# Dilated scores by two query tiles, split lows on Pool, the last head pair's weights spread by TensorE, and an earlier first load of branch weights, in a three-branch encoder block

## The chip, the cores and the metric

The kernel runs on one core of a Trainium2 chip. The profile names its engines: TensorE (PE, with its weight loads as PEld), VectorE (DVE), ScalarE (ACT), GpSimd (POOL, here "Pool") and SyncE (SP), which here only issues DMA. Each takes its own instructions in order; they wait for each other through semaphores. The metric is device microseconds of one execution, as the median of several runs. All data are float32. Matrix products that have to be exact are made as three products of a value's high and low part (h*h, h*l, l*h): a "split" is one ScalarE copy that rounds to the high part, and one subtraction that leaves the low part.

## The reference, cut to what matters

One block over 1024 tokens of width 1024. `h = rms_norm(x)`, one wide projection, three mixers, each gated by a SiLU and projected back, merged by sigmoid gates, projected by `w_out`, normalised and added to `x`. The change lies in the first mixer and in the products that run beside it:

```python
for gi, (window, dil) in enumerate(((128, 1), (512, 4), (2048, 16))):
    o_g, lse_g = dilated_window_attention(aq[gi], ak[gi], av[gi], window, dil)   # 8 heads of 64
wts = softmax(stack(lses), axis=0)                # over the three groups, per token and head
oa  = einsum('gbsh,gbshd->bshd', wts, stack(outs))
ya = (oa * silu(ga)) @ w_br_a
yb = (ob * silu(gb)) @ w_br_b
ym = (om * silu(gm)) @ w_br_m
merged = gates[0] * ya + gates[1] * yb + gates[2] * ym
x = x + rms_norm(merged @ w_out)
```

In each group a query sees the keys at `t + j*dil` with `|j| <= window/(2*dil)`: after sorting tokens by class modulo `dil`, a band of 64 to each side, or, in the third group, all 64 tokens of its class.

## The kernel before, in words

The program runs in stages: projections and cross-attention, grouped-query attention, the values, then the rotated queries and keys together with the merge gates (25 "pairs" of column blocks), then the dilated stage, the first branch's products, and the output projection. The change touches the end of the fourth stage, all of the dilated stage, and the way into the products after it.

**Order.** Every engine's order in these stages is written out by hand: it is the order in which the Python code emits instructions. `weave` (around line 180) mixes two generators: the dense work of `run_items` and an attention generator. Each yields a cost. After each yield it goes on with the dense side if the attention's share `a / att_cost` has reached the dense share `d / dc`, else with the attention. In the dilated stage the dense work is 16 units of 24 matmuls (`add_y`, units 0 to 7 the cross-attention branch, 8 to 15 the grouped-query branch), `dc` = 384 x 216. `att_cost` is the last line of the stage's pacing (`weave(16, every(), ...)`): 7000 + 12 x 9500 + 5000 + 33000 = 159000. The constants stand at the bottom: SOFT 1000, JOINED 300, LAG 3, FIRST_PAD 7000, LAST_PAD 1000. Small pieces of a unit wait in the list `pend`, one popped every third matmul: at a unit's start the load of the next unit's gate (`th_load`), the load of the weights of the unit after it (`y_load`), and the next unit's weight split (`y_split`, high part on ScalarE L1335, low part on Pool L1336); at the end of each half the evacuation (`y_evac`: VectorE L1351 or L1353 out of the PSUM bank `d`, of which there are two, and for units from 8 on an addition on Pool, L1354).

**A cycle.** There are four head pairs and three groups, so twelve items, in the order pair 0 group 0, 1, 2, pair 1 group 0, and so on; an item's cycle has eight steps T, one for each tile of 128 queries. `plan` writes a cycle as a list of pieces. At each step: `soft(T)` (VectorE L1564 adds the mask to the scores in PSUM and takes the minimum of the negated scores, ScalarE L1565 makes the exponential and its sum), `trans(T - 3)` (TensorE transposes the probabilities, VectorE copies them to `app`, L1603 or L1578), a piece of the combination of an earlier pair (`combining`), and loads or splits (`tokens`). `scores(0)` makes the scores of tiles 0 to 3 in the four `s1` banks (two heads, two tiles in a bank), `scores(1)` those of tiles 4 to 7. `joined` puts `scores(1)` behind the previous item's second `pv` at step 3, and the next item's `scores(0)` behind the own first `pv` at step 7. `pv` multiplies with the values into a PSUM bank, and ScalarE copies to `og` (L1632; four buffers). At step 2 `stats` transposes the previous item's minima and sums, and eight or four DMAs (L1647 to L1658) store them to `std` in DRAM, sorted by class.

**Combining a pair.** When a pair's third item is finished, `ready` (step 3 of the next cycle) starts `combine`: `fetch` reads the pair's statistics from `std`, `shares` and `weights` make the softmax over the groups on small tiles, `put` stores it to `wgd`, `get` reads it back spread over 64 rows for each head (`wgt`), `weigh` multiplies each group's `og` and adds them up (Pool, L1796 and L1798), `gate` multiplies with 0.5 and the SiLU gate (VectorE, L1801), `store` keeps or stores the result. `STEP_T` gives the step of each piece, shares first, counted on through the following cycles. For the last pair there is no following cycle: `ending` makes the same pieces one after the other on VectorE, with the DMAs on ScalarE's queue, and then splits the result into `hh[3]` and `hl[3]`.

**The low parts.** The grouped-query branch's operands are loaded and split during the second to sixth cycle (`b_load`, `b_high` L1832, `b_low` L1836 on VectorE); those of the dilated branch that are ready (pairs 0, 1, 2) in the last cycle (`dl_high` L1843, `dl_low` L1846 on VectorE).

**Into and out of the stage.** In the last pass of the loop over the 25 pairs (`n == last`), SP issues `op_load(hi)` (eight loads of the cross-attention operands; four of them take buffers from `kr`, a rotation of ten), `qk_first`, then `y_load(0)`. `c_add` and `c_fin` take more `kr` buffers for the merge gates that end there. After `weave`, units 16 to 18 run with the first three operand tiles (`y_part(m, range(3))`, L1944), then with the fourth.

## Time and profile before

| | |
|---|---|
| median of 3 runs | 1467.03 us (1465.35 to 1470.9) |
| the profiled execution | 1466.1 us, its span 1464.3 us |
| busy share of the span | PE 95%, PEld 76%, DVE 71%, ACT 45%, POOL 41% |
| chain of waits, by engine | PE 75%, DVE 6%, DMA 6%, POOL 5%, issue 3%, ACT 2%, SP's queue 2% |
| `soft` on VectorE, L1564 | 192 instructions, mean 323 ns |
| `soft` on ScalarE, L1565 | 192 activations, mean 422 ns, each with an accumulator read of 187 ns |
| first `soft` starts, last `soft` starts | 1079.3 us, 1275.9 us |
| last unit of `add_y`, first `y_part` matmul | 1319.1 us, 1326.3 us |

The page cuts the span into 40 slices of 36.6 us; a digit is the busy share of a slice in tenths. In a list of groups the columns are: line, engine, operation, tiles written and read, shapes, count; busy us and mean ns of one; idle time just before them and what ended it. In an order of time a line starts with start and duration in us; what stands in brackets is how long the engine was idle before, and what released it. In a list of waits: who waited, for whom, us in all, times, the longest.

### The profile page before, as it was taken

The page shows a single profiled execution, that of the slowest core. Times are in us where ns is not written, and L with a number is a line of the kernel's source. Part 1 is how long each engine was busy: PE and PEld are TensorE (multiplying, and loading weights), DVE is VectorE, ACT ScalarE, POOL GpSimd, SP SyncE. Part 2 cuts the span into 40 slices and gives each one's busy share as a digit, 9 for nine tenths or more (in the row PEclk, how much of TensorE's full clock was granted, in tenths as well). Part 3 has the DMA queues.
Part 4 walks back from the last instruction along what each step waited for, and adds up shares of the span by engine and source line. Part 5 has one row for each costly group of instructions (what it writes and reads, how often), then busy time and mean ns, then how long its engine had stood idle before and what let it go on. Part 6 is the DMA issues. An engine that isn't in the chain of part 4 may idle for free.

```text
span 1464.3 us, 21835 instructions
## 1 busy us (share of the span) xinstructions
PE 1386.2 (95%) x7768; PEld 1113.6 (76%) x7768; DVE 1034.6 (71%) x1805; ACT 659.7 (45%) x1377; POOL 601.3 (41%) x457
## 2 busy tenths in 40 slices
PE   7999999999999999999999999999979898939897
PEld 7799986666666889888888888888857676727786
DVE  7768678677762887677787766777856665644977
ACT  6544366666554453333333333333346555502332
POOL 1416604676654003445555544555400424625303
PEclk9999999999999999999999999999989999979999
DMA  6347432232203795142333333333555676653355
GB/s 237 100 159 260 142 115 94 79 98 89 74 25 123 236 285 175 69 145 82 113 108 115 115 107 109 115 101 119 176 213 184 198 203 213 168 145 120 135 213 173
DMA packets 121341, 209.74 MB, mean 143 GB/s; under 512 B 33616, under 2 KB 62096, under 8 KB 121232
## 3 DMA queue, kind: packets, MB, share of 16 engines
q1 hardware_dynamic: 110160, 192.75, 41.3%
q10 hardware_dynamic: 11072, 15.59, 3.1%
q8 instruction: 61, 1.00, 0.3%
q14 instruction: 48, 0.39, 0.1%
HBM read 143.97 MB, written 64.32 MB: 142 GB/s over the span
## 4 chain that ended last, share of the span: by engine, by line
PE 75%; DVE 6%; DMA 6%; POOL 5%; issue 3%; ACT 2%; SPq 2%; DVEq 0%; ACTq 0%; POOLq 0%
PE s L1298 32%; PE s L1210 4%; PE s L2030 4%; PE ov L797 3%; PE s L1259 3%; PE d L145 3%; PE d L143 3%; PE d L147 3%; PE d L1859 2%; PE s L782 2%; PE s L781 2%; PE tr L763 2%; PE d L2030 1%; DMA wgt<-wgd 1%; PE d L538 1%
## 5 line engine op out<-in xcount | busy, mean ns | idle before, releaser
L788 POOL TENSOR_TENSOR bl<-bl,bp 128x512 f32<-128x512 f32 x96 | 130.8, 1362 | 54.3 <-ACT bp L784 48.9
L1298 PE MATMUL s<-hh,vS 128*128 128x512 f32 x400 | 133.6, 395 | 0.0
L1298 PE MATMUL s<-vA,vS 128*128 128x512 f32 x450 | 106.6, 390 | 0.0
L1565 ACT ACTIVATE pra<-pra,sts 128x192 f32<-128x192 f32 (+2 forms) x192 | 80.8, 422 | 54.4 <-DVE sts L1564 47.0
L106 DVE TENSOR_TENSOR vS<-vot,vS 128x512 fp32r<-128x512 f32 x75 | 85.6, 1143 | 19.9 <-ACT vS L105 19.9
L1298 PEld LDWEIGHTS s<-vA,vS 128*128 128x128 f32 x450 | 84.5, 188 | 18.3
L784 ACT ACTIVATE bp<-s 128x512 f32<-128x512 f32 x128 | 75.8, 596 | 43.2 <-PE s L782 42.2
L764 DVE TENSOR_REDUCE bn<-tr 128x1 f32<-128x512 f32 x128 | 84.8, 683 | 12.0 <-PE tr L763 10.8
L143 PE MATMUL d<-hh,wh 128*128 128x512 f32 x224 | 89.3, 399 | 2.4 <-DVE fth L216 2.4
L147 PE MATMUL d<-hh,wl 128*128 128x512 f32 x224 | 89.4, 399 | 0.0
L1298 PEld LDWEIGHTS s<-hh,vS 128*128 128x128 f32 x400 | 75.3, 188 | 18.3 <-DVE vS L106 0.4
L145 PE MATMUL d<-hl,wh 128*128 128x512 f32 x224 | 88.9, 397 | 0.0
L1336 POOL TENSOR_TENSOR wh<-wr,wh 128x512 fp32r<-128x512 f32 x19 | 26.6, 1401 | 132.6 <-ACT wh L1335 132.6
L1564 DVE CUSTOM_DVE_ANT_0 pra<-s,mask 128x192 f32<-128x192 f32 (+2 forms) x192 | 54.6, 323 | 37.1 <-PE s L1552 17.7
L1298 PE MATMUL s<-hl,vS 128*128 128x512 f32 x200 | 79.1, 395 | 0.0
L1298 PE MATMUL s<-hh,wh 128*128 128x512 f32 x200 | 78.4, 392 | 0.0
L1298 PE MATMUL s<-hh,wl 128*128 128x512 f32 x200 | 78.4, 392 | 0.0
L1298 PE MATMUL s<-hl,wh 128*128 128x512 f32 x200 | 77.8, 389 | 0.0
L1859 PE MATMUL d<-bh,wh 128*128 128x512 f32 x128 | 47.5, 435 | 25.1 <-DVE wl L1353 25.1
L1302 ACT ACTIVATE vv<-s 128x512 f32<-128x512 f32 x50 | 30.0, 599 | 86.0 <-PE s L1298 58.1
L1354 POOL TENSOR_TENSOR acc<-acc,wl 128x512 f32<-128x512 f32 (+1 forms) x23 | 41.2, 1794 | 48.7 <-DVE wl L1353 48.5
L797 PE MATMUL ov<-bp,VS 128*64 128x512 f32 x256 | 58.5, 598 | 0.0
(591 smaller groups left out, 4082.7 us busy)
## 6 DMA issues: line engine op xcount, KB each, us to landing
wr<-in_wu SPq DMA_DIRECT2D x40, 512.0 KB
vA<-in_wu SPq DMA_DIRECT2D x24, 512.0 KB
qkd<-ko SPq DMA_DIRECT2D x96, 128.0 KB
wl<-thd SPq DMA_DIRECT2D x24, 512.0 KB
wos<-os SPq DMA_DIRECT2D x12, 512.0 KB
aq<-qkd SPq DMA_DIRECT2D x12, 512.0 KB
ak<-qkd SPq DMA_DIRECT2D x12, 512.0 KB
wr<-in_wbr SPq DMA_DIRECT2D x24, 256.0 KB
```

The source lines that it names most:

```text
L106: V.tensor_tensor(dst_l, src, dst_h.bitcast(F32), op=OP.subtract)
L143: PE.matmul(dst, wh[:, k, :], hh[k][:, t], start=k == 0, stop=False)
L145: PE.matmul(dst, wh[:, k, :], hl[k][:, t], start=False, stop=False)
L147: PE.matmul(dst, wl[:, k, :], hh[k][:, t], start=False, stop=k == 7)
L764: fp["last"] = V.tensor_reduce(st[i]["n"][:, j, c:c + 1], s, axis=AX.X, op=OP.min)
L784: A.activation(pp, s, AF.Exp, scale=-1.0)
L788: G.tensor_tensor(lsum[i % 2], lsum[i % 2], pp, op=OP.add)
L797: PE.matmul(o[e * 64:e * 64 + 64], VS[:, kt, kv], d.pop(kt), start=kt < 2, stop=kt >= NT - 2)
L1298: PE.matmul(BANK[n, c], a, b, start=k == 0 and q == 0 and not more, stop=k == 3 and q == 2, skip_group_check=c in "XW")
L1565: A.activation(src, src, AF.Exp, scale=-1.0, bias=bias, accum_out=sts[:, h, 1, T:T + 1])
L1859: PE.matmul(ps_, a, b, start=k == 0 and q == 0, stop=k == 3 and q == 2)
L2030: PE.matmul(dst[:, e[0]:e[1]], a, b, start=k == 0 and q == 0, stop=k == 3 and q == 2)
```

## The change

- **Scores.** `scores` makes two tiles a call. The four calls stand at step 5 and 7 of the cycle before (tiles 0 to 3) and at steps 1 and 3 of the own cycle; `joined` is gone, and the costs are divided.
- **Lows and gates.** `b_low` and `dl_low` (but for the last operand) move from VectorE to Pool, `b_high` and `dl_high` go by halves, spread over the steps of a cycle. `gate` of pairs 0 to 2 moves to Pool; its factor 0.5 goes into `weights`. In `STEP_T`, `get` goes from step 0 of the next cycle to step 7, the gate from step 4 to step 1.
- **The last pair.** Its third item writes its statistics straight into `c3`. Those of the first two are read back from DRAM by four loads into `rows` at step 6 of the last cycle, transposed by TensorE into `c3`. `shares_3` makes the softmax over groups, transposes it to 48 rows (group, head, tile), and multiplies it with a 0/1 pattern into a 48 x 1024 tile. `wide` spreads it to 128 rows by a matmul with a second 0/1 pattern; `first_two` and `third` multiply the `og` tiles with it out of PSUM by halves of 512, add them and apply the gate, on VectorE. The last `stats`, `fetch`, `put` and `get` are gone.
- **Pacing.** `att_cost` becomes 136000 (33000 -> 10000), and the padding of the last steps is halved.
- **The first load.** `y_load(0)` stands ahead of `op_load(hi)`. In the last pair of column blocks, `c_add` and `c_fin` take other buffers than those of `kr`.

```diff
@@ c_add, c_fin
-        r = RV[n, u, t] = kr()
+        r = RV[n, u, t] = kr() if n < last or n == last and (u, t) == (0, 0) else SF[(1 - u) * 2]
...
-        r = kr() if ps_ is not None else RV.pop((n, u, t))
+        r = RV.pop((n, u, t)) if ps_ is None else kr() if n < last else p1
@@ the loop over pairs, n == last
+            y_load(0)
             op_load(hi)
             op_split(lo, 0)
             op_split(lo, 1)
...
             qk_first(0)
-            y_load(0)
             th_load(0)
@@ new constants
+        def pickers():
+            i48 = ident[0:48, 0:48]
+            V.tensor_reduce(pick, i48.rearrange("p (x t) -> p t x", t=NT), axis=AX.X, op=OP.add)
+            V.tensor_reduce(each, i48.rearrange("p (x t) -> p x t", t=NT), axis=AX.X, op=OP.add)
+            V.tensor_copy(spread.rearrange("p g h q -> p (g h) q"), each[:, :, None].to_broadcast([48, 6, 64]))
@@ scores
-                    d["sts"] = cb.tile([P, 2, 2, NT], F32, name="sts", bufs=2)
+                    d["sts"] = c3[:, 2] if (p_, g) == (3, 2) else cb.tile([P, 2, 2, NT], F32, name="sts", bufs=2)
-                for j in range(4):
-                    T = 4 * b + j
+                banks = [pss1(), pss1()]
+                for j in range(2):
+                    T = 2 * b + j
@@ tokens
+                if (n, T) == (1, 7):
+                    pickers()
+                if 2 <= n <= 5 and 4 <= T <= 6:
+                    (lambda: b_high(n - 2, lo), lambda: b_high(n - 2, hi), lambda: b_low(n - 2))[T - 4]()
...
+                if n == 11:
+                    if T < 6:
+                        k, z = divmod(T, 3)
+                        dl_high(k, half[z]) if z < 2 else dl_low(k)
+                    else:
+                        dl_high(2, half[T - 6])
                     if T == 4:
-                        DL["g"] = qk.tile([P, S], F32, name="aq", bufs=2)
+                        DL["g"] = cb.tile([P, S], F32, name="wgt", bufs=3)
...
+                        for j in range(4):
+                            nc.sync.dma_start(rows[16 * j:16 * j + 16],
+                                              std[3, j % 2, j // 2].rearrange("s (t a) -> (s t) a", t=NT))
@@ plan
+                if T == 1 and it:
+                    out.append(it["scores"][2])
+                if T == 5 and nxt:
+                    out.append(nxt["scores"][0])
                 if T == 3:
-                    out.append(joined(pre and pre["pv"][1], it and it["scores"][1]))
+                    if pre:
+                        out.append(pre["pv"][1])
                     if it:
+                        out.append(it["scores"][3])
...
                 if T == 7:
-                    out.append(joined(it["pv"][0], nxt and nxt["scores"][0]))
+                    out.append(it["pv"][0])
                     if nxt:
+                        out.append(nxt["scores"][1])
@@ combine
-            def gate(g, gt):
-                V.scalar_tensor_tensor(ogs[g], ogs[g], 0.5, gt, op0=OP.mult, op1=OP.mult)
+            def gate():
+                G.tensor_tensor(ogs[0], ogs[0], c["g"], op=OP.mult)
...
-        STEP_T = (6, 7, 7, 0, 3, 3, 7, 4, 5)
+        STEP_T = (6, 7, 7, 7, 3, 3, 7, 1, 5)
@@ b_low, dl_low
-            V.tensor_tensor(l, l.bitcast(F32), h.bitcast(F32), op=OP.subtract)
+            G.tensor_tensor(l, l.bitcast(F32), h.bitcast(F32), op=OP.subtract)
...
-            V.tensor_tensor(hl[k][:, t], DL[k][:, t], hh[k][:, t].bitcast(F32), op=OP.subtract)
+            (V if k == 3 else G).tensor_tensor(hl[k][:, t], DL[k][:, t], hh[k][:, t].bitcast(F32), op=OP.subtract)
@@ the last pair (shares_3's softmax over groups cut: the same small operations as shares and weights)
+                PE.transpose(tp[:, 0, 0:64], rows, ident[0:64, 0:64])
+                V.tensor_copy(c3[:, 0:2].rearrange("p g h s t -> p (g h s t)"), tp[:, 0, 0:64])
...
+                PE.transpose(tp[0:48, 0, :], C["e"].rearrange("p g h t -> p (g h t)"), ident)
+                C["w"] = wv = cb.tile([P, S], F32, name="wgt", bufs=3)
+                for x in range(2):
+                    t = slice(32 * x, 32 * x + 32)
+                    V.tensor_tensor(wv[0:48, half[x]].rearrange("p (u t z) -> p u t z", t=NT, z=2),
+                                    tp[0:48, 0, :].rearrange("p (z u) -> p u z", z=2)[:, t, None, :].to_broadcast([48, 32, NT, 2]),
+                                    pick[:, None, :, None].to_broadcast([48, 32, NT, 2]), op=OP.mult)
+        def wide(g, x):
+            W3B[g, x] = pst().rearrange("p a b -> p (a b)") if g == 2 else pss1()
+            PE.matmul(W3B[g, x], spread[:, g].rearrange("p h q -> p (h q)"), C["w"][0:48, half[x]], start=True, stop=True)
+        def first_two(x):
+            t = half[x]
+            a, b = C["ogs"]
+            for g, z in enumerate((a, b)):
+                V.tensor_tensor(z[:, t], W3B[g, x], z[:, t], op=OP.mult)
+            V.tensor_tensor(a[:, t], a[:, t], b[:, t], op=OP.add)
+        def third(x):
+            t = half[x]
+            a, b = C["ogs"][0], OG[3, 2]
+            V.tensor_tensor(b[:, t], W3B[2, x], b[:, t], op=OP.mult)
+            V.tensor_tensor(a[:, t], a[:, t], b[:, t], op=OP.add)
+            V.tensor_tensor(a[:, t], a[:, t], DL["g"][:, t], op=OP.mult)
@@ ending, every
+            return [(lambda: [wide(g, 0) for g in range(2)], 300.0), (lambda: [wide(g, 1) for g in range(2)], 300.0),
+                    (lambda: [first_two(0), wide(2, 0)], 1000.0), (lambda: [first_two(1), wide(2, 1)], 1000.0),
+                    (lambda: third(0), 1000.0), (lambda: dl_high(3, lo), 100.0), (lambda: third(1), 1000.0),
+                    (lambda: dl_low(3, lo), 100.0), (lambda: dl_high(3, hi), 100.0), (lambda: dl_low(3, hi), 1000.0),
+                    (out_pool, 100.0), (lambda: [wo_load(nm, k) for nm in ("B11", "B21") for k in range(4)], 500.0)]
...
-                yield cost + LAST_PAD
+                yield cost + LAST_PAD / 2
...
-        weave(16, every(), FIRST_PAD + 12 * (NT * (SOFT + 100.0) + 2 * JOINED + 100.0) + 5 * LAST_PAD + 33000.0)
+        weave(16, every(), FIRST_PAD + 12 * (NT * (SOFT + 100.0) + 2 * JOINED + 100.0) + 5 * LAST_PAD + 10000.0)
```

More of the change, by code (lines that the diff above doesn't have):

```diff
@@ L1468, in block @@
         G.memset(vpart, 0.0)
+        rows = aa.tile([64, P], F32, name="rows")
+        c3 = aa.tile([P, 3, 2, 2, NT], F32, name="c3")
+        pick = aa.tile([48, NT], F32, name="pick")
+        each = aa.tile([48, 6], F32, name="each")
+        spread = aa.tile([48, 3, 2, 64], F32, name="spread")
+        def pickers():
[3 more added lines that the diff above has]
+            V.tensor_copy(spread.rearrange("p g h q -> p (g h) q"), each[:, :, None].to_broadcast([48, 6, 64]))
         def qk_fetch(p_, g):
@@ L1887, in wo_split @@
             split(h, l, l.bitcast(F32))
[L1889 to L1903 removed]
+        C, W3B = {}, {}
```

98 lines of the change are left out of this document (45 added, 53 removed).

## The prediction

> **What bounds the kernel now.** I read the page's slices first, for where TensorE is not full; then windows around the dilated stage, for how much of it is missing there; then each engine's order of time at the two places where it stands, and the waits in between.
>
> ```profile
> span 1464.3 us, 21835 instructions
> ...
> PE   7999999999999999999999999999979898939897
> ```
>
> Slices are 36.6 us. TensorE is full until slice 28 and has one deep hole, the 3 in slice 35 (1281 to 1318). The changed code runs from about 1047 to 1345. Its windows (us; then busy time and count of TensorE, weight loads, VectorE, ScalarE, GpSimd; clock, DMA share, GB/s), and below them the branch matmuls of L1859 alone:
>
> ```profile
> 1079.30:1277.00 197.70, 177.98 (x1835) 143.76 (x1836) 124.24 (x519) 118.69 (x435) 67.07 (x34) 0.96 0.62 186
> 1277.00:1294.70 17.70, 17.07 (x101) 12.99 (x99) 11.03 (x18) 4.20 (x10) 9.52 (x7) 1.00 0.36 101
> 1294.70:1319.10 24.40, 0.00 (x0) 0.00 (x0) 10.01 (x13) 2.41 (x4) 1.29 (x2) 0.58 0.66 177
> 1319.10:1326.30 7.20, 7.16 (x25) 5.74 (x26) 1.78 (x3) 0.00 (x0) 5.41 (x4) 0.77 0.45 147
> 1326.30:1464.30 138.00, 123.91 (x541) 100.91 (x539) 105.38 (x138) 41.64 (x89) 39.41 (x34) 0.96 0.47 162
> ```
>
> ```profile
> 1079.30:1277.00 197.70, 89.52 (x268) 44.99 (x269) 0.96 0.62 186
> 1277.00:1294.70 17.70, 16.06 (x65) 11.64 (x64) 1.00 0.36 101
> 1319.10:1326.30 7.20, 7.16 (x24) 5.54 (x24) 0.77 0.45 147
> ```
>
> The twelve cycles take 197.7 us with TensorE at 90%: there it is nearly the bound. After the last softmax (1277) come 17.7 us of branch matmuls, 24.4 us of nothing, then unit 15. What ends the nothing, in VectorE's and TensorE's order of time:
>
> ```profile
> 1288.39 0.63 DVE L1769 TENSOR_TENSOR cmn<-cpt 128x16 f32<-128x16 f32 x1 [1.21 <-DMA cpt<-std]
> ...
> 1290.74 0.21 DVE L1783 TENSOR_TENSOR ceg<-ceg,cds 128x48 f32<-128x48 f32 x1
> ...
> 1301.04 1.03 DVE L1796 TENSOR_TENSOR og<-og,wgt 128x512 f32<-128x512 f32 x1 [9.50 <-DMA wgt<-wgd]
> 1306.98 1.03 DVE L1796 TENSOR_TENSOR og<-og,wgt 128x512 f32<-128x512 f32 x1 [4.90 <-DMA wgt<-wgd]
> ...
> 1318.32 0.68 DVE L1353 SCALAR_TENSOR_TENSOR wl<-wl,d 128x512 f32<-128x512 f32 x1
> ```
>
> ```profile
> 1319.14 0.76 PE L1859 MATMUL d<-bh,wh 128*128 128x512 f32 x1 [24.50 <-DVE wl L1353]
> 1319.71 0.63 PE L1859 MATMUL d<-bl,wh 128*128 128x512 f32 x1
> ```
>
> VectorE stands three times for the weights that went to DRAM and back (`put`, `get`); the evacuation L1353 of unit 14 is queued behind those multiplies, so both `d` banks stay full and TensorE stops. When it starts again its clock is low: 0.58 and 0.77 in the windows.
>
> **The change, part by part.**
>
> *Start.* `y_load(0)` goes ahead of the eight loads of `op_load(hi)` and two of `qk_first`. SP's, ScalarE's and TensorE's order of time:
>
> ```profile
> 1047.37 0.37 SPq L1318 DMA_DIRECT2D tab<-g2d  x1
> ...
> 1049.83 0.38 SPq L1318 DMA_DIRECT2D vy<-od  x1
> 1056.75 0.32 SPq L1318 DMA_DIRECT2D tab<-g2d  x1
> ...
> 1058.59 0.38 SPq L1330 DMA_DIRECT2D wr<-in_wbr  x1
> ```
>
> ```profile
> 1066.10 0.63 ACT L1335 ACTIVATE wh<-wr 128x512 fp32r<-128x512 f32 x1 [8.20 <-DMA wr<-in_wbr]
> ```
>
> ```profile
> 1066.79 0.80 PE L1859 MATMUL d<-hh,wh 128*128 128x512 f32 x1 [4.81 <-ACT wh L1335]
> ```
>
> The load would be issued at about 1047.4 and, even at the 7.5 us that this one took, be there by 1055; ScalarE is free at 1058. What is late next is the products' own end: TensorE's last one ends at 1066.79 - 4.81 = 1061.98. So unit 0 can gain at most 4.8 us; the low half on VectorE comes after a load that SP issues one slot (0.4 us) later, and I take 3.7. All that follows on VectorE and ScalarE up to the first softmax moves with it. The other buffers of `c_add` and `c_fin` cost nothing: the four that `op_load(hi)` takes are drawn earlier in the rotation, so SP's gap from 1049.83 to 1056.75 stays.
>
> *Pacing.* The constants of the interleaving give the share of branch matmuls issued by the last cycle's end: before (7000+114000)/159000 = 76%, 292 of 384 (the trace: 384-65-24 = 295). After, 121000/136000 = 89%, 342. So 47 more stand inside the cycles; at 16.06/65 = 0.247 us that is +11.6 us of TensorE. It leaves 42 for the tail.
>
> *Score blocks of two tiles.* The waits of VectorE and of TensorE's weight loads inside the cycles (total, times, longest):
>
> ```profile
> DVE pra L1564 <- PE s L1552: 17.7, 11, 2.4
> ...
> DVE pra L1564 <- PE s L1545: 12.5, 8, 2.3
> ```
>
> ```profile
> PEld tr L1624 <- DVE app L1603: 9.4, 8, 2.8
> PEld tr L1591 <- ACT og L1632: 6.1, 3, 3.0
> ...
> PEld s L1552 <- DVE sts L1564: 3.0, 2, 2.3
> ```
>
> The same matmuls run, now issued two tiles ahead of the softmax that reads them, so VectorE's 30.2 us of waits should mostly go. That is no gain by itself, since TensorE is the fuller engine; it counts where it shortens TensorE's 18.5 us above. The extra matmuls also give the others time. Bounds: nothing recovered, or all of TensorE's idle time there, 197.7 - 178.0 = 19.7 us. I take 12, most of what the rows for VectorE's lateness (9.4, 3.0) come to; the `og` wait is Pool's. Net of the cycles: about 0. VectorE's wait for the fetched statistics of pairs 0 to 2 stays as it is.
>
> *Split lows and gates on Pool.* From the groups by form between 1066 and 1320:
>
> ```profile
> L1796 POOL TENSOR_TENSOR og<-og,wgt 128x1024 f32<-128x1024 f32 x9 | 27.2, 3027 | 23.0 <-DMA wgt<-wgd 23.0
> ...
> L1336 POOL TENSOR_TENSOR wh<-wr,wh 128x512 fp32r<-128x512 f32 x15 | 21.0, 1400 | 122.7 <-ACT wh L1335 122.7
> ...
> L1798 POOL TENSOR_TENSOR og<-og 128x1024 f32<-128x1024 f32 x6 | 15.1, 2517 | 0.5
> L1351 DVE SCALAR_TENSOR_TENSOR acc<-wl,d 128x512 f32<-128x512 f32 x16 | 10.9, 679 | 0.0
> L1836 DVE TENSOR_TENSOR bl<-bl,bh 128x1024 fp32r<-128x1024 f32 x4 | 6.4, 1611 | 0.4 <-ACT bh L1832 0.4
> L1846 DVE TENSOR_TENSOR hl<-hl,hh 128x1024 fp32r<-128x1024 f32 x2 | 5.2, 2592 | 0.3 <-ACT hh L1843 0.3
> L1801 DVE SCALAR_TENSOR_TENSOR og<-og,wgt 128x1024 f32<-128x1024 f32 x3 | 3.7, 1227 | 0.0
> L1846 DVE TENSOR_TENSOR hl<-og,hh 128x1024 fp32r<-128x1024 f32 x1 | 1.3, 1299 | 0.9 <-ACT hh L1843 0.9
> ```
>
> VectorE loses 6.4 + 5.2 + 1.3 + 3.7 = 16.6 us; Pool gains four lows, three gates, three lows of the last operand, 10 x 2.5 = 25 us, on 67 in 197.7. On average there is room. Queued behind them on Pool are the weight lows L1336. One is issued at the ninth matmul of a unit and needed 15 matmuls later, some 9 us (314 matmuls in 197.7 us are 24 in 15). Where a pair's weighing (3 x 3.0 + 2 x 2.5 us) meets a low, a gate and a weight low, 20 us fall into the 12 between step 3 of one cycle and step 1 of the next, so Pool is late by up to 8: covered, with one to spare. Each us beyond that is paid at three places.
>
> The first L1846 took twice the second; the first ran beside Pool's additions. The Trainium skill (GPSIMD Engine Reference, Specifications) says why this speaks against the change: Pool shares its SBUF interface with VectorE, and contends with VectorE instructions that have two SBUF inputs. By the trace that holds here. By that rule the six two-input additions and gates that the new tail has on VectorE would take 1.3 instead of 0.7, 4 us more; the sum without it leaves them at 0.7.
>
> *Weights of pairs 0 to 2.* `get` moves from the next cycle's first step to right behind `put`, past one load of values on SP: earlier by 1 to 3 us, hidden for the same reason that Pool's wait on it mostly is. The gate at step 1 instead of 4 stores earlier; nobody waits. `pickers` is three small VectorE instructions, under 1 us once. `b_high` and `dl_high` in halves cost two more instructions' start. The four loads of `rows` stand on SP behind the eight statistics stores of pair 3, group 1; if they land late, the transpose of `rows` holds TensorE, 0 to 3 us, and I take 1.5.
>
> *Tail.* Gone: the statistics transposed, stored, fetched, put and got. New on TensorE: two transposes and six matmuls of 48 rows by 512 columns. Their bound is a row of another stage of the chain, plain fp32 in two halves side by side:
>
> ```profile
> 454.19 3.58 PE ov L797 x16
> ```
>
> that is 0.45 us for a full-width one, 2.7 for six. TensorE then has 42 x 0.247 = 10.4, the last transposes and products 2, and 2.7: 15.1 us. Beside it VectorE has the softmax over groups (1288.39 to 1290.95, 2.6 us), two spreads (0.7 as L1351, or 1.0 as L1796 above: 2), twelve half-tile products at 0.68 (8.2), four evacuations (2.7): 15.5 us, with six hand-overs between TensorE, ScalarE and VectorE ahead of the first spread product. TensorE will wait in them: 1.5 for `rows`, about 1 at each of three more, so 5 (bounds 2 and 11). Tail 20 us, where 1277 to 1326.3 is 49.3: -29.3. What follows the spread products, ten half-tile steps, lies beside the first 54 matmuls of units 16 to 18, which need only three of four operand tiles (some 12 us).
>
> *After it.* The window from 1326.3 stays, but the eight `wB` loads ran inside the hole:
>
> ```profile
> 1293.83 5.11 SPq L1883 DMA_DIRECT2D wB<-wod  x5
> ```
>
> Now they come at the tail's end. ScalarE reaches the weight split of unit 17 only behind the last `dl_high`: 2 us, and the load of 18 stands behind eight loads on SP: 0 to 4. I take +3 (bounds 0 and 6). If TensorE stands there too long, its clock falls again: the Trainium skill (TensorE: Matmul & The Clock Gate, What's actually happening) has a few busy us at half rate before full speed returns, and the rows at 1319 agree, 0.57 us from start to start against 0.247.
>
> **Sum.** -3.7 + 0 - 29.3 + 3 = -30 on the profiled execution's 1466.1 us: 1436. That execution lies 0.9 below the median of the runs, which is less than this sum can tell.
>
> **Rivals.**
> - *TensorE is the bound inside the cycles.* Nothing is recovered: +11.6; the tail takes 26 (-23), the rest +5, the start -2: -8.4 to -12, about 1456. For it: 90% busy. Against: the two late engines' waits in its rows.
> - *The cycles tighten.* Recovered 19.7 less 11.6 (-8), tail 17 (-32), start -4, nothing after: -44, 1422. For it: 30.2 us of VectorE waits at exactly the blocks that are split. Against: TensorE's own order.
> - *Slower: TensorE stands at the new meeting points.* It now needs the softmax of the tile just before at steps 1 and 5 of each cycle, 24 places more. From 1.25 us at each the 30 us are gone; at the 2.3 us that the longest such wait took it is 55, so 1491. For it: TensorE's order is fixed. Against: only two such waits in twelve cycles, and a wait there lets VectorE run on.
> - *The hole stays,* because `rows` or the chain to `wide` is as late as the round trip: 1462 to 1467. Against: no DRAM access remains after the last softmax.
>
> **How the numbers follow.** Forecast (1428 to 1446) 0.48, bound cycles (1447 to 1459) 0.22, tight cycles (1412 to 1427) 0.16, slower 0.10, hole stays 0.04. Faster is the first three, 0.86; 0.5% of the time is 7.3 us, about what a measurement of this kernel can tell from no change. The range 1417 to 1457 leaves out the last two and the outer parts of the two beside the forecast.
>
> **What would show it.** Right: first softmax near 1075.6; the cycles 190 to 205 us; no TensorE gap over 4 us after the last softmax, the first L1944 matmul about 20 us behind it, and then about 141 us. Wrong: TensorE waiting on `sts` in most cycles (slower), on `wh` of Pool in cycles 4, 7, 10 (Pool late), on `rows`, or over 10 us lost after the first L1944.

## The result, and the profile after

The changed kernel took 1450.25 us (median of 4 runs, 1449.14 to 1454.56) beside 1467.30 for the kernel before: a ratio of 0.9886, with a 95% interval of 0.9858 to 0.9915. That is 17 us faster where 30 were forecast, between the forecast (1436) and the rival of the bound cycles (1456). It lies in that rival's range (1447 to 1459, chance 0.22), not in the forecast's own (1428 to 1446, 0.48). The profiled execution took 1454.56, 4.3 above its median; 3.0 us later than before it reaches the end of the products, where the other kernels below lie at 1061.9 to 1064.2.

Five events cut the trace into stages: the end of the products (the last matmul of L1298), the first softmax, the last softmax (each by its start; the prediction cut the old tail at that softmax's end, 1.1 us later), the first `y_part` matmul, the end.

| us | products' end | first softmax | last softmax | first y_part | end | start | cycles | tail | after |
|---|---|---|---|---|---|---|---|---|---|
| before | 1062.0 | 1079.3 | 1275.9 | 1326.3 | 1464.3 | 17.3 | 196.6 | 50.4 | 138.0 |
| changed | 1065.0 | 1077.4 | 1281.1 | 1315.3 | 1452.7 | 12.4 | 203.7 | 34.2 | 137.4 |
| difference | +3.0 | | | | -11.6 | -4.9 | +7.1 | -16.2 | -0.6 |

The page of the changed kernel, slices of 36.3 us:

```profile
span 1452.7 us, 21831 instructions
...
PE   7999999999999999999999999999989989989897
```

The deep hole is gone. Its windows by stage (us; then busy time and count of TensorE, weight loads, VectorE, ScalarE, GpSimd; clock, DMA share, GB/s):

```profile
1077.40:1281.10 203.70, 194.30 (x1872) 153.32 (x1873) 112.55 (x515) 120.71 (x443) 88.33 (x47) 0.98 0.64 190
1281.10:1289.90 8.80, 2.21 (x37) 1.62 (x33) 0.63 (x5) 2.24 (x6) 8.12 (x5) 0.80 0.50 150
1289.90:1300.00 10.10, 10.10 (x59) 6.47 (x60) 6.92 (x17) 1.81 (x3) 3.82 (x3) 0.83 0.21 67
1300.00:1315.30 15.30, 15.30 (x30) 7.62 (x29) 8.85 (x13) 1.78 (x3) 2.96 (x2) 0.55 0.49 160
1315.30:1452.70 137.40, 123.50 (x541) 100.58 (x539) 105.30 (x138) 41.74 (x89) 39.35 (x34) 0.98 0.48 165
```

The tail now has one stand of TensorE, 6.6 us, and is full of matmuls behind it, but those run at a clock of 0.83 and then 0.55. The same view for the branch matmuls (L1870) alone, cycles and tail:

```profile
1077.40:1281.10 203.70, 104.42 (x321) 54.44 (x321) 0.98 0.64 190
1281.10:1315.30 34.20, 16.83 (x43) 10.51 (x43) 0.70 0.41 130
```

and for the spread matmuls (L1936, twelve records for six matmuls):

```profile
1281.10:1315.30 34.20, 9.28 (x12) 2.49 (x12) 0.70 0.41 130
```

TensorE's order of time in the tail:

```profile
1282.91 0.40 PE L1870 MATMUL d<-bh,wh 128*128 128x512 f32 x1
1289.89 0.34 PE L1907 MATMUL tr<-cs,rows 64*128 64x64 f32 x1 [6.58 <-DMA rows<-std]
...
1297.08 1.98 PE L1936 MATMUL s<-wgt,spread 48*128 48x512 f32 x4
1298.99 0.50 PE L1870 MATMUL d<-bl,wh 128*128 128x512 f32 x1
...
1303.64 2.07 PE L1936 MATMUL tr<-wgt,spread 48*128 48x512 f32 x2
1305.65 0.79 PE L1870 MATMUL d<-bl,wh 128*128 128x512 f32 x1
```

Two spread matmuls take 1.91 us from start to the next start at full clock (1.00 from 1297 to 1300), and one takes 2.01 once the clock is down (0.50 from 1301 to 1312).

Why `rows` is late stands in SP's order of time:

```profile
1269.40 1.26 SPq L1504 DMA_DIRECT2D avs<-vdr  x2
1276.25 0.33 SPq L1343 DMA_DIRECT2D wl<-thd  x1
1276.67 1.22 SPq L1330 DMA_DIRECT2D wr<-in_wbr  x1
1277.98 5.18 SPq L1665 DMA_DIRECT2D std<-sr  x8
...
1285.26 1.81 SPq L1709 DMA_DIRECT2D rows<-std  x4
```

and in SP's waits between 1268 and 1280 (total, times, longest):

```profile
SPq L1343 <- POOL acc L1354: 5.5, 1, 5.5
```

SP stands 5.5 us, until 1276.25, at a gate load (`th_load`, L1343), whose buffer comes free only when GpSimd has added a branch half (L1354). The eight statistics stores and the four loads of `rows` queue behind it.

In the cycles TensorE stands twice for long, 3.8 us in cycle 6 and 3.2 in cycle 9, counted from 0 (the prediction, counting from 1, would call them 7 and 10). VectorE's and TensorE's order of time at the first:

```profile
1195.37 0.17 DVE L1782 TENSOR_TENSOR cmn<-cpt 128x16 f32<-128x16 f32 x1 [5.36 <-DMA cpt<-std]
```

```profile
1196.33 1.26 PE L1562 MATMUL s<-ak,aq 64*128 64x128 f32 x12 [3.78 <-DVE sts L1574]
```

VectorE waits for the statistics that come back from DRAM, the softmax is queued behind that wait, and the next scores need the softmax's result.

### The profile page after: what moved, and what is told of

It reads as the page before. It is cut to its first block, busy times and chain, and to the rows that moved or that the text cites. A ratio compares the mean times of both kernels' runs of the same rounds, so it can differ in the third digit from the quotient of the medians.

```text
span 1452.7 us, 21831 instructions
## 1 busy us (share of the span) xinstructions
PE 1405.7 (97%) x7781; PEld 1120.3 (77%) x7781; DVE 1016.4 (70%) x1800; ACT 660.3 (45%) x1383; POOL 620.8 (43%) x467
## 4 chain that ended last, share of the span: by engine, by line
PE 77%; DMA 7%; DVE 6%; POOL 3%; ACT 3%; issue 3%; SPq 2%; DVEq 0%; ACTq 0%; POOLq 0%
PE s L1298 32%; PE d L1870 6%; PE s L2085 4%; PE ov L797 3%; PE s L1259 3%; PE d L147 3%; PE d L145 3%; PE d L143 3%; PE s L1562 2%; PE s L782 2%; PE s L781 2%; PE tr L1634 2%; PE tr L763 2%; PE d L2085 1%; DMA vrt<-rld 1%
## 5 line engine op out<-in xcount | busy, mean ns | idle before, releaser
L1298 PE MATMUL s<-hh,vS 128*128 128x512 f32 x400 | 133.6, 395 | 0.0
L1298 PE MATMUL s<-vA,vS 128*128 128x512 f32 x450 | 106.6, 390 | 0.0
L1298 PEld LDWEIGHTS s<-vA,vS 128*128 128x128 f32 x450 | 84.5, 188 | 18.3
L1575 ACT ACTIVATE pra<-pra,sts 128x192 f32<-128x192 f32 (+2 forms) x176 | 75.4, 429 | 45.1 <-DVE sts L1574 44.5
L764 DVE TENSOR_REDUCE bn<-tr 128x1 f32<-128x512 f32 x128 | 84.8, 683 | 12.1 <-PE tr L763 11.0
L1298 PEld LDWEIGHTS s<-hh,vS 128*128 128x128 f32 x400 | 75.3, 188 | 18.4 <-DVE vS L106 0.4
L1298 PE MATMUL s<-hl,vS 128*128 128x512 f32 x200 | 79.1, 395 | 0.0
L1298 PE MATMUL s<-hh,wh 128*128 128x512 f32 x200 | 78.4, 392 | 0.0
L1298 PE MATMUL s<-hh,wl 128*128 128x512 f32 x200 | 78.4, 392 | 0.0
L1298 PE MATMUL s<-hl,wh 128*128 128x512 f32 x200 | 77.8, 389 | 0.0
L1613 DVE COPY app<-tr 128x384 f32<-128x384 f32 (+1 forms) x64 | 38.8, 607 | 47.9 <-PE tr L1601 31.1
L1336 POOL TENSOR_TENSOR wh<-wr,wh 128x512 fp32r<-128x512 f32 x19 | 24.9, 1309 | 106.2 <-ACT wh L1335 86.8
L1354 POOL TENSOR_TENSOR acc<-acc,wl 128x512 f32<-128x512 f32 (+1 forms) x23 | 40.3, 1751 | 45.3 <-DVE wl L1353 45.3
L797 PE MATMUL ov<-bp,VS 128*64 128x512 f32 x256 | 58.5, 598 | 0.0
L1044 POOL TENSOR_TENSOR vot<-vot,vA 128x512 f32<-128x512 f32 x12 | 19.0, 1584 | 91.1 <-DVE vS L106 91.1
```

Source lines behind the costliest of these rows:

```text
L764: fp["last"] = V.tensor_reduce(st[i]["n"][:, j, c:c + 1], s, axis=AX.X, op=OP.min)
L797: PE.matmul(o[e * 64:e * 64 + 64], VS[:, kt, kv], d.pop(kt), start=kt < 2, stop=kt >= NT - 2)
L1298: PE.matmul(BANK[n, c], a, b, start=k == 0 and q == 0 and not more, stop=k == 3 and q == 2, skip_group_check=c in "XW")
L1575: A.activation(src, src, AF.Exp, scale=-1.0, bias=bias, accum_out=sts[:, h, 1, T:T + 1])
```

## The experiments

All are edits of the changed kernel. Stages are those of the profiled execution, times and ratios those of the runs.

| kernel | median us | ratio to before, 95% | start | cycles | tail | after |
|---|---|---|---|---|---|---|
| changed | 1450.25 | 0.9886 (0.9858 to 0.9915) | 12.4 | 203.7 | 34.2 | 137.4 |
| gate load later | 1439.81 | 0.9813 (0.9787 to 0.9839) | 11.2 | 195.6 | 31.6 | 138.7 |
| shares at 7 | 1443.43 | 0.9833 (0.9806 to 0.9859) | 9.4 | 198.9 | 34.1 | 137.3 |
| scores by four | 1444.08 | 0.9841 (0.9810 to 0.9873) | 9.3 | 199.9 | 33.7 | 138.6 |
| lows on VectorE | 1449.84 | 0.9879 (0.9859 to 0.9899) | 10.0 | 211.3 | 25.9 | 138.5 |
| both moves | 1436.49 | 0.9790 (0.9769 to 0.9812) | 10.7 | 195.4 | 32.1 | 137.4 |
| both, scores by four | 1437.15 | 0.9793 (0.9773 to 0.9814) | 10.3 | 193.6 | 32.7 | 137.7 |
| start undone | 1456.14 | 0.9920 (0.9904 to 0.9937) | 18.0 | 200.4 | 33.6 | 137.3 |
| spread in one pass | 1443.64 | 0.9843 (0.9824 to 0.9862) | 10.7 | 201.7 | 24.1 | 140.9 |
| both, two queues | 1443.71 | 0.9819 (0.9792 to 0.9846) | 9.2 | 198.6 | 33.3 | 137.4 |
| both, two queues, split spread | 1435.95 | 0.9779 (0.9757 to 0.9801) | 9.5 | 198.8 | 24.3 | 139.6 |
| both, old pacing | 1442.03 | 0.9822 (0.9800 to 0.9843) | 9.5 | 188.9 | 42.7 | 137.7 |
| both, split spread, rows first | 1435.49 | 0.9791 (0.9760 to 0.9822) | 9.7 | 195.2 | 23.8 | 140.3 |

Single executions of one kernel lie up to 10 us apart (1435.15 to 1444.92 for the two queues), so stages of single profiles are read to some 3 us.

**Gate load later.** The gate load goes behind the evacuation of a unit's first half.

```diff
-                pend.extend([lambda: th_load(m + 1), lambda: y_load(m + 2), lambda: y_split(m + 1, G)])
+                pend.extend([lambda: y_load(m + 2), lambda: y_split(m + 1, G)])
...
                     pend.append(lambda t=t, ps_=ps_: y_evac(m, t, ps_))
+                    if t is lo:
+                        pend.append(lambda: th_load(m + 1))
```

> The changed kernel, with each unit's load of the next unit's gate (th_load) issued behind the evacuation of its first half instead of at its start. Theory A: the 6.6 us that TensorE waits for `rows` in the tail come from SP, which stands 6.9 us at a gate load whose buffer Pool has not freed yet, so that the statistics' stores and the `rows` loads behind it on SP are late. By A the gate load finds its buffer free, `rows` lands some 6 us earlier, TensorE's wait for it falls below 2 us, the half clock that follows it is shorter, and the time falls by 6 to 10 us against the changed kernel, to 1440 to 1445. Rival: the stores and loads of the statistics are themselves the long part (eight stores of 5.2 us and the landing of four loads); then the wait stays above 4 us and the time within 3 us of 1450.

10.4 us less than the changed kernel, the time of theory A, but not where it put it: the wait for `rows` fell only from 6.6 to 4.4 us, as the rival has it, and the larger part came in the cycles. Waits of VectorE there, changed kernel first, then this one:

```profile
DVE cmn L1782 <- DMA cpt<-std: 10.7, 3, 5.4
```

```profile
DVE cmn L1782 <- DMA cpt<-std: 3.7, 3, 1.7
```

With that wait TensorE's two long stands at the scores went too. That the fetch of the statistics queues on SP behind a gate load is shown for one of the two places: in cycle 9 of the changed kernel SP stands 1.8 us for L1354 at a gate load ahead of the fetch. In cycle 6 it stands at none; there the statistics stores ahead of the fetch wait 0.9 to 1.2 us for each of four earlier DMAs, a gate load among them. Why the fetch came in time there stays open.

**Shares at 7.** The combining's first piece, which waits for that fetch, at step 7 instead of 6: `STEP_T = (7, 7, 7, 7, 3, 3, 7, 1, 5)`.

> The changed kernel, with the softmax over groups of pairs 0 to 2 one step later (step 7 instead of 6), behind the last softmax tile of the cycle. Theory B: in the cycles 6 and 9 TensorE stands 4.1 and 3.4 us at the next scores, which now need the softmax tiles behind the wait of VectorE for the fetched statistics (5.4 us), so the score blocks of two tiles turned a wait of VectorE into one of TensorE. By B both waits go, the two long cycles (25.1 and 24.2 us) lose about 4 us each, and the time falls by 5 to 9 us against the changed kernel, to 1441 to 1445. Rival: VectorE's wait only moves one step on and stops the first tile of the next cycle; TensorE then waits as long for its transposes, and the time stays within 3 us of 1450.

6.8 us less, as theory B has it; VectorE's wait for the fetch fell to 4.3 us, TensorE's longest stands at the scores to 1.6 and 1.4, and the wait for `rows` stayed (6.5). So VectorE's wait for the fetch was the cause of the long stands in the cycles, and it has nothing to do with `rows`.

**Scores by four.** The blocks of two score tiles joined again, at steps 3 and 7, as before the change.

```diff
-                if T == 1 and it:
-                    out.append(it["scores"][2])
-                if T == 5 and nxt:
-                    out.append(nxt["scores"][0])
...
+                        out.append(it["scores"][2])
                         out.append(it["scores"][3])
...
+                        out.append(nxt["scores"][0])
                         out.append(nxt["scores"][1])
```

> The changed kernel, with the scores again made four tiles at a time, at steps 3 and 7. If the blocks of two tiles are worth what the prediction put on them (about 12 us less waiting of TensorE in the cycles), the time rises by 6 to 14 us against the changed kernel, to 1456 to 1464. Theory B's stronger form: the new meeting points cost as much as the earlier scores save; then it stays within 4 us of 1450, the 4.1 and 3.4 us waits of TensorE for the softmax are gone, and VectorE's waits for scores are back at some 30 us.

6.2 us less, where 6 to 14 more or no change were expected: the split was to recover most of 12, and by this run it costs. The intervals of the two ratios overlap, though, and the two stands at the scores (8.0 us together) are still there.

**Both moves, with and without the split.** To settle it, the two moves together, with blocks of two and of four on the same chip.

> Both moves at once: the gate load behind the evacuation of a unit's first half, and the combining's first piece at step 7 instead of 6. Theory A (both cure the same late fetch of the statistics, SP standing at the gate load): the gains, 10.4 and 6.8 us, do not add: 1437 to 1441, cycles near 195. Theory B (two separate losses, one of SP and one of the order of the pieces): they add, 1431 to 1435, cycles near 190.

> The same with the scores in blocks of four tiles again, as before the change. Theory A (blocks of two cost TensorE time at each change from dense matmuls to scores and back): 3 to 6 us less than the kernel with both moves, at equal clock, and the cycles shorter by as much. Theory B (the block of two recovers waits of VectorE and with them time, and the gain seen with the late fetch in place was noise): equal within 1 us, or 3 to 12 us more, with VectorE's waits for scores back at near 30 us.

1436.49 and 1437.15: with the late fetch out of the way the size of the blocks makes no difference. The two moves win 13.8 us together, between one gain (10.4) and the sum (17.2), so they cure the same delay in part. The waits of VectorE over 1070 to 1285, the changed kernel, then its waits for transposes in the kernel before:

```profile
DVE app L1613 <- PE tr L1601: 31.1, 25, 3.2
DVE app L1588 <- PE tr L1586: 30.7, 15, 3.2
DVE app L1613 <- PE tr L1610: 16.8, 13, 3.1
...
DVE pra L1574 <- PE s L1562: 1.4, 1, 1.4
```

```profile
DVE app L1603 <- PE tr L1591: 13.9, 13, 3.0
...
DVE app L1603 <- PE tr L1600: 10.0, 7, 2.6
...
DVE app L1578 <- PE tr L1576: 8.0, 8, 1.3
```

The waits for scores did go, from 30.2 to 1.4 us; those for transposes rose from 31.9 to 78.6. VectorE waits for TensorE either way. With both moves and blocks of four, 28.9 us for scores and 32.7 for transposes are back, in the same time.

**Lows on VectorE.** The ten operations that went to GpSimd (three gates, seven low halves) back on VectorE.

> The changed kernel, with the ten moved operations (four and three low parts, three gates) back on VectorE. Theory A: Pool's lateness behind them is what holds the gate loads on SP and so `rows`; then Pool is free some 7 us earlier in the last cycle, TensorE's wait for `rows` falls by 3 us or more, and the time falls by 2 to 6 us against the changed kernel. Rival: VectorE needs the room in the cycles more than Pool does (16.6 us of work back on it); then the time rises by 3 us or more.

The same time, otherwise made up: cycles 7.6 us longer, tail 8.3 shorter, the wait for `rows` 1.5 us. Neither theory has the time, and the shorter wait is not theory A's either: the loads of `rows` are issued 209.5 us behind the first softmax here and 207.9 in the changed kernel, so they do not come sooner; what waits for them comes later. Moving work to GpSimd won in the cycles what it lost in the tail.

**Start undone.** `y_load(0)` behind `qk_first` again, buffers of `c_add` and `c_fin` as before.

> The changed kernel without its start: the load of the first branch weights behind the gate loads again, and the buffers of c_add and c_fin as before. Theory A (the start is worth what its profiles show, 17.3 us from the last product to the first softmax before and 9.3 to 12.4 with the change): first softmax 5 to 8 us later, 1455 to 1458. Theory B (the step as priced, 3.7): 1454. Theory C (what is won at the start is given back in the first cycle): within 1.5 us of 1450.

5.9 us more (by the ratios 5.0), and the first softmax 18.0 us behind the products. Theory A. TensorE's order of time here, where the stand ahead of the first branch matmul is back:

```profile
1068.17 0.80 PE L1870 MATMUL d<-hh,wh 128*128 128x512 f32 x1 [5.50 <-ACT wh L1335]
```

In the changed kernel it stands 4.0 us at the third branch matmul instead, for the low half of the weights; the difference, 1.5, is less than the gain. Whether the rest comes from the buffers or from VectorE's order was not separated.

**Spread in one pass.** The six spread matmuls in fp32r, the rounded type that the high and low parts have. The weights of the last pair are rounded for it; that is all that is left out.

```diff
-        spread = aa.tile([48, 3, 2, 64], F32, name="spread")
+        spread = aa.tile([48, 3, 2, 64], R, name="spread")
...
-                    V.tensor_tensor(wv[0:48, half[x]].rearrange("p (u t z) -> p u t z", t=NT, z=2),
+                    V.tensor_tensor(wv.bitcast(R)[0:48, half[x]].rearrange("p (u t z) -> p u t z", t=NT, z=2),
...
-            PE.matmul(W3B[g, x], spread[:, g].rearrange("p h q -> p (h q)"), C["w"][0:48, half[x]], start=True, stop=True)
+            PE.matmul(W3B[g, x], spread[:, g].rearrange("p h q -> p (h q)"), C["w"].bitcast(R)[0:48, half[x]], start=True, stop=True)
```

> The six spread matmuls in fp32r, one pass each instead of plain fp32; the weights of the last head pair are rounded to fp32r for it, so the last quarter of the first branch's operand is less exact. Theory A (the six matmuls' own 9.3 us stand on the path): they take under 2 us, the tail falls from 34.3 to 27 to 29, 1443 to 1445. Theory B (VectorE's products, which read them, are as long as TensorE's work): the tail falls by under 2 us and TensorE stands longer after them, 1448 to 1450.

6.6 us less, as theory A has it, and the tail fell by 10.1 us, more than the matmuls' own time (9.3 to 2.5). Windows of its tail, and L1936 in it alone:

```profile
1276.30:1281.90 5.60, 0.41 (x3) 0.09 (x1) 0.13 (x1) 0.54 (x1) 5.60 (x4) 0.93 0.59 166
1281.90:1290.00 8.10, 8.10 (x52) 6.09 (x52) 5.54 (x14) 0.77 (x3) 3.53 (x4) 0.63 0.23 83
1290.00:1298.50 8.50, 8.50 (x30) 5.28 (x31) 7.46 (x12) 2.19 (x3) 1.34 (x2) 1.00 0.75 240
```

```profile
1274.40:1298.50 24.10, 2.46 (x6) 0.95 (x6) 0.86 0.48 152
```

The low clock behind the stand at `rows` is still there (0.63). The second low stretch, behind the spread matmuls, is gone: 1.00 where the changed kernel has 0.55. The stage after it grew by 3.5 us.

**Two queues.** On top of both moves, four of the eight statistics stores issued by ScalarE (`E = nc.scalar if (p_, g) == (3, 1) and h else nc.sync`).

> The kernel with both moves, and of the eight statistics stores of head pair 3's second group four issued by ScalarE, so that SP reaches the four loads of rows some 3 us sooner. Theory A (the stand at rows is time lost, and its half clock too): the stand falls from 4.1 to under 1.5 us, the tail from 32.1 to 27 to 29, 1432 to 1434. Theory B (the work behind it is bound by VectorE or by the spread matmuls): tail 31 to 33, 1436 to 1438. For the second stretch of low clock, at the spread matmuls: if it comes from the stand at rows it goes with it; if it comes from the plain fp32 matmuls themselves it stays, with the clock at 0.55 to 0.65 behind the first four of them.

A miss: 1443.71, and the wait for `rows` is 5.3 us, not shorter. SP's waits between 1258 and 1276 say why:

```profile
SPq L1665 <- DMA std<-sr: 4.7, 1, 4.7
```

By the profile SP's own four stores waited 4.7 us, until 1267.20, for a landing of the same stores; ScalarE had issued its four by 1266.4, so it is most likely theirs. The stand did not get shorter, so its price stays open, and so does the second question by this run: the low clock at the plain spread matmuls is still there,

```profile
1290.00:1304.30 14.30, 14.30 (x28) 7.54 (x27) 7.63 (x12) 1.26 (x2) 1.66 (x1) 0.53 0.43 141
```

but so is the stand. What answers it are two other runs: in one pass the stand is 5.2 us and no second stretch follows, and with the lows on VectorE the stand is 1.5 us and the stretch is there (last section).

**Two queues, split spread.** The spread matmuls in fp32r with the weights as a high and a low half, so that nothing is rounded away but the last bits.

```diff
-                C["w"] = wv = cb.tile([P, S], F32, name="wgt", bufs=3)
+                C["w"] = [cb.tile([P, S], F32, name="wgt", bufs=3).bitcast(R) for _ in "hl"]
...
+                    wv = aa.tile([P, 512], F32, name="pra", bufs=5)[0:48]
...
+                    split(*[z[0:48, half[x]] for z in C["w"]], wv)
...
-            PE.matmul(W3B[g, x], spread[:, g].rearrange("p h q -> p (h q)"), C["w"][0:48, half[x]], start=True, stop=True)
+            for y, w in enumerate(C["w"]):
+                PE.matmul(W3B[g, x], spread[:, g].rearrange("p h q -> p (h q)"), w[0:48, half[x]], start=y == 0, stop=y == 1)
```

> The same, and the spread matmuls in fp32r with the weights split into a high and a low half (twelve matmuls of one pass, for six in plain fp32), at two more steps of ScalarE and two of VectorE ahead of them. Theory A (the six plain matmuls cost their own 9 us and the half clock behind them): the twelve take near 3 us, the clock stays at full behind them, the tail falls by 5 to 7 us more against the kernel with two queues, 1427 to 1431. Theory B (the chain from VectorE's weights to its products binds once the matmuls are short): the two extra steps are paid, the tail falls by 0 to 3.

7.8 us less than the kernel with two queues by the medians, 5.9 by the ratios, whose intervals overlap a little; 0.5 less than both moves alone. The 1427 to 1431 had counted on the two queues to win 3 to 4 first. Two windows of its tail, behind the stand at `rows` and on to the end, and the twelve spread matmuls:

```profile
1278.00:1283.00 5.00, 5.00 (x14) 3.64 (x14) 4.27 (x10) 0.24 (x1) 2.67 (x2) 0.50 0.46 157
1283.00:1295.80 12.80, 12.80 (x75) 8.56 (x74) 11.14 (x19) 3.28 (x5) 4.28 (x3) 0.97 0.40 133
```

```profile
1271.50:1295.80 24.30, 3.84 (x12) 1.92 (x12) 0.86 0.51 167
```

Again no second stretch of low clock: 0.97 on to the end.

**Old pacing.** Both moves, with the constant of the interleaving back at 33000.

> The kernel with both moves, with the pacing constant at 33000 as before the change, so that some 47 branch matmuls stand in the tail again instead of in the cycles. Theory A (the cycles have 12 us of TensorE's idle time that the 47 fill, as the forecast had it): the cycles stay within 3 us of 195.4, the tail grows by 10 to 12, 1445 to 1449. Theory B (TensorE is the bound in the cycles): the cycles fall by 9 to 12 us to near 185, the tail grows as much, 1435 to 1439.

Between the theories. The cycles alone, all work and then L1870, with both moves and then with the old pacing:

```profile
1074.20:1269.60 195.40, 191.35 (x1870) 150.91 (x1872) 111.70 (x513) 121.44 (x444) 88.56 (x47) 1.00 0.66 197
...
1074.20:1269.60 195.40, 102.48 (x321) 53.28 (x321) 1.00 0.66 197
```

```profile
1071.50:1260.40 188.90, 180.81 (x1821) 142.18 (x1821) 110.81 (x511) 118.50 (x438) 80.58 (x41) 1.00 0.67 196
...
1071.50:1260.40 188.90, 89.84 (x272) 43.83 (x270) 1.00 0.67 196
```

49 more branch matmuls, worth 49 x 0.247 = 12.1 us, lengthen the cycles by 6.5 and shorten the tail by 10.6. So about half of their time is found in TensorE's idle time, and the pacing is worth some 5 us of the total (the two intervals still touch, 0.9769 to 0.9812 and 0.9800 to 0.9843).

**Both moves, split spread, rows first.** All stores on SP, and the load of pair 3's gates (512 KB) behind the four loads of `rows` instead of ahead of them.

> Both moves and the split spread matmuls, all statistics stores on SP again, and the load of pair 3's gates (512 KB) put behind the four loads of rows in SP's order instead of ahead of them. Theory A (ScalarE's 3.2 us of issuing cost the cycles what SP won, and rows land late because of the megabyte of gates that the same queue carries ahead of them): cycles 195 to 197, the stand at rows from 4.1 us to 2 or less, tail 22 to 23, 1428 to 1432. Theory B (the rows' own chain, stores landing and loads landing, sets their time): the stand stays at 4 to 5 us, 1433 to 1436.

The waits of TensorE in it from 1060 to 1325:

```profile
PE s L1562 <- DVE sts L1574: 3.3, 9, 0.6
PE tr L1927 <- DVE ceg L1924: 2.5, 1, 2.5
PE tr L1908 <- DMA rows<-std: 2.2, 1, 2.2
```

The wait for `rows` is 2.2 us, near what theory A has, but VectorE's small operations behind it (`ceg`) hold TensorE for 2.5 more, and the median, 1435.49, is theory B's. Its median is the lowest of all, but it is not told apart from both moves alone (1436.49, and the ratios are the same): its profiled execution has a tail 8.3 us shorter, yet the medians differ by 1.0, and part of the gain is given back after it (140.3 for 137.4). What makes up the rest was not found, so the 6.6 us of the spread in one pass are not shown to add to those of the two moves.

## Why the forecast was right in sign and too large

**Start: -3.7 forecast, -4.9 in the profiles, 5 to 6 by undoing it.** Right, a little small. What the forecast named as late next, the low half on VectorE behind the last load of `op_load`, is what TensorE stood for (4.0 us).

**Cycles: 0 forecast, +7.1 measured.** The added work was near the forecast: 53 more branch matmuls instead of 47, 13.1 us. The recovery was half of the 12 taken: 196.6 + 13.1 - 203.7 = 6.0. With both moves it is 196.6 + 13.1 - 195.4 = 14.3, so the idle time was there to be had. But it did not come from the split, as the forecast had it: with blocks of four the cycles are 193.6. The measured cycles lie midway between the forecast and the rival of the bound cycles, in which nothing was recovered. The step that failed is "VectorE's wait for the fetched statistics of pairs 0 to 2 stays as it is": it went from 8.6 to 10.7 us, and TensorE stood 3.8 us behind the longest one and 3.2 behind the next (2.1 at most before). The step's other half failed too: the split score blocks were to recover most of it, and are worth nothing by themselves. VectorE's waits for scores only turned into waits for transposes. TensorE did stand at scores, as in the rival that forecast a slower kernel: 9.3 us in 8 waits, most of it at two places, where that rival needed some 24.

**Lows on GpSimd: covered, but not at every place.** The ten operations took 9.5 + 7.2 + 4.7 + 2.4 = 23.8 us, beside 25 forecast, and in the changed kernel TensorE's waits show none for a weight low of GpSimd. The forecast looked at the weight lows (L1336) as what is queued behind them. What was queued was also L1354, which frees the gate buffer that SP waits for, and SP's statistics stores behind that. This chain, GpSimd to SP to DRAM to TensorE, was not in the sum. That the gate load's place on SP costs is shown by moving it (10.4 us). That it is GpSimd's new work that made it cost is not shown. SP's last wait for L1354 ahead of those stores, in the kernel before and with the lows on VectorE, beside 5.5 us in the changed kernel:

```profile
SPq L1343 <- POOL acc L1354: 2.3, 1, 2.3
```

```profile
SPq L1343 <- POOL acc L1354: 3.4, 1, 3.4
```

So the wait grew by 3.2 us and 2.1 of them go with the lows, but `rows` came no sooner for it, as said above. The new pacing also shifts the units, and with them the gate loads, against the cycles; the two were not separated.

**Tail: 20 forecast, 34.2 measured.** By the forecast's own terms:

| term | forecast us | measured us |
|---|---|---|
| branch matmuls | 42 x 0.247 = 10.4 | 43, 16.8 busy |
| spread matmuls | 2.7 | 9.3 |
| wait for `rows` | 1.5 (0 to 3) | 6.6 |
| other waits | 3.5 | none over 1 us |
| transposes, products | 2 | 1.5 (the rest of 34.2) |

Three terms were mis-sized, one was too cautious. The price of the spread matmuls came from a row (L797) that was read wrongly. Its 16 records are eight matmuls, because a plain fp32 matmul leaves two records (12 for the six spread ones); that makes four pairs side by side at 0.90 us, not eight at 0.45, and six would cost 5.4 us. The first two spread matmuls measure 0.95 each; what is left of the 9.3 us is the low clock. The Trainium skill (FP8 and Floating Point Precision, TensorE Precision Notes) says that true fp32 makes four passes; 4 x 0.247 is 0.99, an estimate, and the trace agrees. The branch matmuls were priced at full clock. The forecast spoke of the low clock only behind the tail; here some 17 of the 25 us behind the stand run at half clock.

The 4 us that the rule of the Trainium skill (GPSIMD Engine Reference, Specifications) would have cost on VectorE's six two-input additions and gates did not come, because GpSimd hardly ran beside them. Five of the six took 0.69 us with GpSimd idle; the one that ran beside it took 1.00, which is not against the rule:

```profile
1309.23 1.28 POOL L1336 TENSOR_TENSOR wh<-wr,wh 128x512 fp32r<-128x512 f32 x1 [11.49 <-ACT wh L1335]
```

```profile
1310.06 1.00 DVE L1949 TENSOR_TENSOR og<-og 128x512 f32<-128x512 f32 x1
```

**After: +3 forecast, -0.6 measured.** Not wrong about the mechanism: where the tail is 10 us shorter, this stage is 2 to 3.5 us longer (139.6 to 140.9), and TensorE has a new wait of 1.0 to 1.6 us for a weight low there, the late split that the forecast named. That the long tail of the changed kernel hides it is argued from these runs.

**The sum.** That 1450 is near the rival of the bound cycles is partly luck: the rival had 11.6 us for the cycles (7.1 measured), a tail of 26 (34.2) and 5 behind it (-0.6), and these errors partly cancel. That both moves bring the kernel to 1436, the forecast's number, is luck too: its tail is 32.1 us and not 20, and its start, 10.7 for 17.3, wins 6.6 and not 3.7.

## What to carry to other kernels

For each load in an in-order queue, ask whose work frees the buffer that it waits for: here a load that waits for such a buffer stands ahead of the statistics stores, and everything behind it, down to the loads that were to be quick, pays. Take the price of a new instruction from a row with the same type and the same tile, find out from the kernel how many instructions the row's records are, and price the work behind a stand at the clock that the profile shows after stands. A wait that goes away on an engine that is not the bound turns up in the next row of the same engine's waits, and is not time won.

## What the hardware showed unexpectedly

TensorE's clock fell to half without TensorE standing still. In the changed kernel the clock is back at 1.00 by 1294, after the stand at `rows`; the spread matmuls (plain fp32, 48 rows by 512 columns) start at 1297.08, and some 3 us later it falls, with TensorE shown busy throughout. TensorE alone (busy, count; clock, DMA share, GB/s), the changed kernel and then the one with the lows on VectorE, where the spread matmuls start at 1293.35 and no low clock comes before them:

```profile
1299.00:1300.00 1.00, 1.00 (x4) 1.00 0.78 266
...
1302.00:1304.00 2.00, 2.00 (x4) 0.50 0.40 151
```

```profile
1294.00:1296.00 2.00, 2.00 (x6) 1.00 0.28 53
...
1298.00:1300.00 2.00, 2.00 (x4) 0.50 0.70 241
```

In the kernel with one pass, and in that with the split, no such stretch follows (1.00 and 0.97), though both have the stand at `rows` and the low clock behind that. So it comes with the plain fp32 spread matmuls. Plain fp32 alone does not do it in every form: in the kernel before, those of L797 (128 rows, pairs side by side, 3.6 us at a time) lie between 238 and 458 us, and the clock is 1.00 in each of six windows over that stretch. The Trainium skill (TensorE: Matmul & The Clock Gate, What's actually happening) has the clock set by how busy TensorE has been recently; whether the 48 rows, the length of the run or something else makes these count for less, no run here shows.
